# A four-layer sequence trunk: norm factors in PSUM and the state-space tables in wider products

## The chip, the cores and the metric

The kernel runs on one core of one Trainium2 chip. The metric is the device time of one execution in microseconds (us). Its engines each work through a queue of their own in order: TensorE (PE in the profile, PEld for its weight loads), VectorE (DVE), ScalarE (ACT), GpSimd (POOL) and SyncE (SP), which here issues the DMAs. All matmul products land in PSUM, eight banks of 2 KB per partition; everything else lies in SBUF.

## The reference

Four layers over a stream of 512 positions with 1024 channels, float32. Each layer has a token mixer (stick-breaking attention, a diagonal state-space layer, a convolution, attention again) and a SwiGLU channel mixer; each of these eight sub-layers stands between two RMS norms with scales and shifts computed from a conditioning vector.

```python
def rms_norm(x, g):
    y = xf * lax.rsqrt(jnp.mean(xf * xf, axis=-1, keepdims=True) + EPS)
    return y * g

for layer in range(DEPTH):
    sh_m, sc_m, g_m, sh_f, sc_f, g_f = split(mod_all[layer], 6)
    u = modulate(rms_norm(h, norm_g[layer, 0]), sh_m, sc_m)
    m = mixer(u)                       # attention, s5_layer or conformer_conv
    h = h + g_m * rms_norm(m, norm_g[layer, 1])
    u = modulate(rms_norm(h, norm_g[layer, 2]), sh_f, sc_f)
    f = (silu(u @ w_gate) * (u @ w_up)) @ w_down
    h = h + g_f * rms_norm(f, norm_g[layer, 3])

def s5_layer(u, ...):                  # 64 groups of 16 channels, 64 complex states each
    ar, ai = exp(lr*dt)*cos(li*dt), exp(lr*dt)*sin(li*dt)
    er, ei = ((a - 1) / lam)           # complex
    bb = e * b
    x[t] = a * x[t-1] + bb @ u[t]      # complex scan over the positions
    y = real(c @ x) + d_skip * u
    ...
```

## The kernel before, in words

**Layout.** The residual stream h lies in SBUF as eight chunks of 128 channels by 512 positions. A float32 product is made of three matmuls on a high and a low part of each operand (`mm3`, L219), both rounded for the fast format; the parts are made by ScalarE (a cast, L237) and by DVE or POOL (a subtraction, L238).

**Phases.** Each of the eight sub-layers is a phase: a first part (`first`), a body (`mid`), a last part (`last`), a norm of its input (`pre`) and of its output (`post`). `cross` (L296) leads from one phase to the next in two halves of 256 positions: while the norms of half A run, PE does the last blocks of half B; while the norms of half B run, it does the first blocks of the next phase on half A. The order of PE's matmuls there is written out by hand, and a norm says after how many microseconds of other PE work its own matmul stands (`yield wait`).

**Norms.** `add_square` (L433) squares a chunk on ScalarE and adds it to one of two sums, the even ones on DVE, the odd ones on POOL. `rstd` (L413) sums over partitions with a matmul of ones into a PSUM bank and makes the factor R in SBUF: a reciprocal root and a square on ScalarE, two instructions on DVE (L425, L427). `postnorm` (L470) scales each of eight chunks by R on DVE (L475) in place and adds it to h (L479), even chunks on DVE, odd ones on POOL. `pre_r` (L444) squares h again, and `prenorm` (L451) scales h by R into a scratch tile in SBUF (DVE, L462), from which ScalarE makes the high part (L463) and DVE the low part (L465) or, for odd chunks in a crossing, ScalarE and POOL (L467, L468).

**Tables.** The state-space layer works on four positions at a time with tables made of its parameters. They are made during the channel mixer of layer 0 (`ffn`, L482; its body is one dense run of 36 blocks of weights) and stored to DRAM. `s5_small` (L929) makes the 4096 values of a, e and of the rotations in a chain of small DVE instructions; `s5_tables(c)` (L1042) makes the tables of one of eight chunks: powers of a times B and C by repeated complex products on POOL (`cmul`, L1025; products L1035 to L1037 and L1039, sums L1038 and L1040), memsets and copies into block-diagonal tiles `bd` and `od` (ScalarE, L1072, L1073), eight transposes (L1077) and eight small matmuls (L1086) on PE, the rotation products on POOL, and seven stores on SyncE's queue (L1080, L1081, L1098, L1107).

**Order.** These tasks stand in a list (`todo`), together with 59 tasks of the conditioning (`mod_block`, L372: a 512 KB fetch and a DVE instruction L376), a table task at every fifth place (L1283); after each block of the body two tasks of the list are issued (`some`). But this is the program's order alone. The order in every engine's queue is set before the run by a planner with a model of durations (`TC`, L15), which takes at each step the instruction that is first in program order among those that it believes ready. At run time each engine follows that order, whatever comes late.

## Time and profile before

| | us |
|---|---|
| median of 3 runs | 2720.92 |
| lowest, highest | 2720.15, 2722.32 |
| the profiled execution | 2724.05 |
| its span, first to last instruction | 2722.3 |
| PE busy | 2480.0 |
| DVE, ACT, POOL busy | 1707.7, 1194.9, 798.1 |

The profiled execution is longer than its span by what lies around the first and last instruction. Busy time is an average over stages with different limits; the rows further down are taken from the stages that the change touches. "Idle before" is the time in which an engine stood still ahead of an instruction, with what released it. PEclk is the granted TensorE clock as a share of full speed.

### The profile page before, as it was taken

To read this page: it belongs to the slowest core of one execution; us is meant where nothing else is said; L and a number is where in the kernel's file an instruction comes from. 1 tells how busy PE (TensorE), PEld (TensorE's weight loads), DVE (VectorE), ACT (ScalarE), POOL (GpSimd) and SP (SyncE) were. 2 spreads that over 40 slices of the span, in tenths; PEclk is the share of its full clock that TensorE was granted. 3 is DMA by queue.
4 is the path that set the end of the run, shared out by engine and by line. 5 is a ranking of instruction groups with operands and counts; after the bars stand their busy time and mean duration, and the time that the engine had idled before them with its cause. 6 is when DMAs were issued, how large, how long until landed. Compare 5 with 4: busy or idle time off the path is not lost.

```text
span 2722.3 us, 35325 instructions
## 1 busy us (share of the span) xinstructions
PE 2480.0 (91%) x12903; PEld 2064.2 (76%) x12903; DVE 1707.7 (63%) x2693; ACT 1194.9 (44%) x2291; POOL 798.1 (29%) x1171
## 2 busy tenths in 40 slices
PE   7898999889866989999988879999998999899998
PEld 5676887666666888888876668888886777888887
DVE  8799767455469465555469986656364887632335
ACT  3577442433346454222356564222243776522222
POOL 4123314999825230000037752000021222300001
PEclk9999999998988999999989989999999999999999
DMA  7423226556636223755301211656221113122331
GB/s 257 149 92 107 76 89 215 174 195 208 233 115 187 69 86 113 235 184 193 127 30 39 70 63 47 224 200 233 96 91 62 40 43 103 42 93 93 93 100 56
DMA packets 115326, 335.09 MB, mean 123 GB/s; under 512 B 12112, under 2 KB 26960, under 8 KB 115152
## 3 DMA queue, kind: packets, MB, share of 16 engines
q1 hardware_dynamic: 115152, 332.84, 37.0%
q8 instruction: 101, 1.65, 0.2%
q14 instruction: 73, 0.60, 0.1%
HBM read 314.18 MB, written 18.61 MB: 122 GB/s over the span
## 4 chain that ended last, share of the span: by engine, by line
PE 61%; DVE 17%; POOL 11%; ACT 4%; issue 4%; DMA 2%; SPq 0%; DVEq 0%; POOLq 0%; ACTq 0%
PE mm L216 56%; PE aux L216 4%; DVE m L475 3%; DVE aux L812 2%; POOL x L1039 2%; POOL x L1037 2%; POOL x L1038 1%; POOL x L1040 1%; DVE raw L376 1%; DVE wlo L238 1%; POOL cm L1036 1%; DVE h L479 1%; POOL cm L1035 1%; PE aux L593 1%; DVE t L462 1%
## 5 line engine op out<-in xcount | busy, mean ns | idle before, releaser
L216 PE MATMUL mm<-u,whi 128*128 128x512 f32 (+1 forms) x3568 | 1078.7, 385 | 16.7 <-DVE cum L745 12.6
L216 PEld LDWEIGHTS mm<-u,whi 128*128 128x128 f32 x3568 | 659.6, 191 | 159.7 <-DVE cum L745 14.6
L237 ACT ACTIVATE whi<-raw 128x1024 fp32r<-128x1024 f32 (+3 forms) x392 | 344.3, 896 | 828.8 <-PE mm L216 519.0
L216 PE MATMUL mm<-u,wlo 128*128 128x512 f32 (+1 forms) x1784 | 687.3, 386 | 0.0
L238 DVE TENSOR_TENSOR wlo<-raw,whi 128x1024 fp32r<-128x1024 f32 (+2 forms) x302 | 357.8, 1187 | 394.8 <-ACT whi L237 391.6
L216 PE MATMUL mm<-hid,whi 128*128 128x512 f32 (+1 forms) x1832 | 506.3, 363 | 1.3 <-ACT whi L237 0.7
L216 PEld LDWEIGHTS mm<-u,wlo 128*128 128x128 f32 x1784 | 340.1, 191 | 70.0 <-issue 1.0
L216 PEld LDWEIGHTS mm<-hid,whi 128*128 128x128 f32 x1832 | 328.4, 191 | 60.2 <-issue 1.0
L216 PE MATMUL mm<-hid,wlo 128*128 128x512 f32 (+1 forms) x916 | 332.3, 364 | 1.8 <-DVE wlo L238 1.8
L441 POOL TENSOR_TENSOR accp<-accp,sq 128x256 f32<-128x256 f32 (+1 forms) x47 | 36.8, 784 | 817.8 <-ACT sq L440 817.5
L376 DVE SCALAR_TENSOR_TENSOR raw<-raw,cb 128x1024 f32<-128x1024 f32 x192 | 240.4, 1274 | 37.9 <-DMA raw<-in_w_modT_dram 36.8
L238 POOL TENSOR_TENSOR wlo<-raw,whi 128x512 fp32r<-128x512 f32 (+1 forms) x90 | 117.8, 1326 | 369.7 <-ACT whi L237 369.7
L495 DVE TENSOR_TENSOR g<-g,mm 128x512 f32<-128x512 f32 (+1 forms) x100 | 61.6, 622 | 253.8 <-PE mm L216 223.4
L216 PEld LDWEIGHTS mm<-hid,wlo 128*128 128x128 f32 x916 | 174.7, 191 | 29.9 <-DVE wlo L238 2.5
L216 PE MATMUL mm<-u,x 128*128 128x256 f32 (+1 forms) x832 | 130.0, 293 | 23.6 <-ACT u L463 8.8
L216 PE MATMUL mm<-hid,u 128*128 128x256 f32 x1104 | 143.3, 291 | 1.5 <-DVE m L757 1.5
L216 PEld LDWEIGHTS mm<-hid,u 128*128 128x128 f32 x1104 | 140.3, 199 | 2.6 <-DVE m L757 1.7
L216 PEld LDWEIGHTS mm<-u,x 128*128 128x128 f32 x832 | 113.9, 199 | 30.1 <-ACT u L463 10.7
L781 POOL TENSOR_TENSOR hid<-ident,hid 128x512 fp32r<-128x512 f32 (+1 forms) x17 | 18.5, 1108 | 315.1 <-ACT hid L237 311.6
L509 DVE TENSOR_TENSOR m<-mm,m 128x256 f32<-128x256 f32 (+1 forms) x92 | 47.7, 523 | 87.9 <-PE mm L216 87.9
L807 POOL TENSOR_TENSOR u<-u,t 128x512 f32<-128x512 f32 (+1 forms) x63 | 78.9, 1252 | 33.6 <-ACT t L806 30.6
L812 DVE SCALAR_TENSOR_TENSOR aux<-cum,vec,aux 128x512 f32<-128x512 f32 (+1 forms) x125 | 86.5, 708 | 2.5
(292 smaller groups left out, 3574.8 us busy)
## 6 DMA issues: line engine op xcount, KB each, us to landing
raw<-in_w_modT_dram SPq DMA_DIRECT2D x192, 512.0 KB, 4.4
raw<-in_ffn_w_gate_dram SPq DMA_DIRECT2D x88, 512.0 KB, 4.0
raw<-in_ffn_w_up_dram SPq DMA_DIRECT2D x88, 512.0 KB, 3.4
raw<-in_ffn_w_down_dram SPq DMA_DIRECT2D x64, 448.0 KB, 3.9
raw<-in_sb_w_qkv_dram SPq DMA_DIRECT2D x32, 512.0 KB, 3.4
raw<-in_ffn_w_down_dram SPq DMA_DIRECT2D x32, 512.0 KB, 4.6
raw<-in_cv_w_pw_dram SPq DMA_DIRECT2D x24, 512.0 KB, 3.3
s5tab<-x SPq DMA_DIRECT2D x40, 256.0 KB, 3.1
```

The source lines that it names most:

```text
L216: self.queue(self.nc.tensor.matmul(out, lhsT, rhs, **k))
L237: a = self.nc.scalar.activation(hi, src, AF.Copy)
L238: b = (self.nc.gpsimd if pool else self.nc.vector).tensor_tensor(lo, src, hi.bitcast(F32), ALU.subtract)
L376: self.after(nc.vector.scalar_tensor_tensor(raw, raw, 1.0, self.cb, ALU.mult, ALU.mult, accum_out=self.mod[l][:, e : e + 1]), self.mark)
L441: (nc.gpsimd if k % 2 and self.mark else nc.vector).tensor_tensor(acc, acc, sq, ALU.add)
L475: nc.vector.scalar_tensor_tensor(t, t, self.gpost[l][:, s, k : k + 1], R, ALU.mult, ALU.mult)
L495: self.mark = nc.vector.tensor_tensor(g, g, pu, ALU.mult)
L509: nc.vector.tensor_tensor(m[ob][:, sl], ps, m[ob][:, sl], ALU.add)
L807: nc.gpsimd.tensor_tensor(ap, ap, x, ALU.add)
L812: nc.vector.scalar_tensor_tensor(c, src(t), wd(k, t), c, ALU.mult, ALU.add)
L1037: TT(oim, are, bim, ALU.mult)
L1039: TT(ore, are, bre, ALU.mult)
```

## The change

It has three parts.

Norms: `rstd` leaves R in the PSUM bank of its sum and hands out the other half of that bank, into which `postnorm` puts the scaled chunk; all additions to h are DVE's. `prenorm` of a half takes a further PSUM bank (`room`) whose two halves hold the scaled chunks in turn; the second scratch of odd chunks stays in SBUF. `add_square` adds chunks 1 to 6 to one sum, on POOL, and leaves the square of chunk 7 by itself for the matmul of ones.

Tables: `s5_small` also makes four powers of a times e and of a; `s5_math` then makes each chunk's tables in two complex products of 256 elements and one of 512 in place of eight of 64 and four of 128. `bd`, `od` and `td` are cleared once and written again for each chunk; ScalarE sets the signs while it copies.

Order: the tables' work is split into `s5_math` (POOL), `s5_place` (ScalarE) and `s5_store` (PE, DVE, stores). The list has the math of chunk c+1 ahead of the placing of c, and the store of c after the math of c+2, just ahead of the placing of c+1. A table task stands at every third place instead of every fifth: 18 table tasks, 77 in all.

```diff
     def rstd(self, accs, n=S, wait=0, out=None):
+        nc = self.nc
+        bank = self.psum("aux")
+        ps = bank[:, :n]
...
         nc.vector.scalar_tensor_tensor(q, ps, EPS, q, ALU.add, ALU.mult)
-        out = r if out is None else out
+        out = ps if out is None else out
         self.step = square, nc.vector.scalar_tensor_tensor(out, q, -3.0, r, ALU.add, ALU.mult)
-        return out
+        return out, bank[:, n : 2 * n] if n < S else None
...
     def add_square(self, accs, src, k, sl=FULL):
-        acc = accs[k % 2][:, sl]
-        if k < 2:
-            return nc.scalar.activation(acc, src, AF.Square)
+        acc = accs[0][:, sl]
+        if k == 0 or k == KC - 1:
+            return nc.scalar.activation(accs[k > 0][:, sl], src, AF.Square)
         sq = self.scratch("sq", sl)
         square = nc.scalar.activation(sq, src, AF.Square)
-        (nc.gpsimd if k % 2 and self.mark else nc.vector).tensor_tensor(acc, acc, sq, ALU.add)
+        (nc.gpsimd if self.mark else nc.vector).tensor_tensor(acc, acc, sq, ALU.add)
         return square
...
     def prenorm(self, l, s, u, sl=FULL, before=None):
-        R = yield from self.pre_r(sl)
+        R, _ = yield from self.pre_r(sl)
+        n = sl.stop - sl.start
+        room = self.psum("aux") if n < S else None
         for k in range(KC):
...
-            t = self.scratch("t", sl)
+            t = self.scratch("t", sl) if room is None else room[:, k % 2 * n : (k % 2 + 1) * n]
             scale = nc.vector.scalar_tensor_tensor(t, self.h[:, k, sl], a, R, ALU.mult, ALU.mult)
             self.step = nc.scalar.activation(hi, t, AF.Identity, bias=b), scale
             if k % 2 == 0 or not self.crossing:
                 nc.vector.scalar_tensor_tensor(lo, t, b, hi.bitcast(F32), ALU.add, ALU.subtract)
             else:
-                nc.scalar.activation(t, t, AF.Identity, bias=b)
-                nc.gpsimd.tensor_tensor(lo, t, hi.bitcast(F32), ALU.subtract)
+                x = self.scratch("t", sl)
+                nc.scalar.activation(x, t, AF.Identity, bias=b)
+                nc.gpsimd.tensor_tensor(lo, x, hi.bitcast(F32), ALU.subtract)
...
     def postnorm(self, l, s, m, accs, sl=FULL, permuted=False):
-        R = yield from self.rstd([a[:, sl] for a in accs], sl.stop - sl.start, 1.6 if sl.start == 0 else 0.4)
+        R, t = yield from self.rstd([a[:, sl] for a in accs], sl.stop - sl.start, 1.6 if sl.start == 0 else 0.4)
         for k in range(KC):
-            t = m[k][:, sl]
-            nc.vector.scalar_tensor_tensor(t, t, self.gpost[l][:, s, k : k + 1], R, ALU.mult, ALU.mult)
+            nc.vector.scalar_tensor_tensor(t, m[k][:, sl], self.gpost[l][:, s, k : k + 1], R, ALU.mult, ALU.mult)
             h = self.h[:, k, sl]
             if permuted:
-                h, t = nat(h), perm(t)
-            (nc.gpsimd if k % 2 else nc.vector).tensor_tensor(h, h, t, ALU.add)
+                nc.vector.tensor_tensor(nat(h), nat(h), perm(t), ALU.add)
+            else:
+                nc.vector.tensor_tensor(h, h, t, ALU.add)
...
-            r = yield from self.rstd(sq, n, 5.0)
+            r, _ = yield from self.rstd(sq, n, 5.0)
...
-        nai = s("nai")
-        nc.vector.tensor_scalar(nai, ai, -1.0, None, ALU.mult)
-        self.s5p = dict(ar=ar, ai=ai, nai=nai, er=er, ei=ei, rho=rho, R0=R0, R1=R1)
+
+        pe, pa = ([t[:, i * P : (i + 1) * P].rearrange("p (j n) -> p j n", j=4) for i in range(2)]
+                  for t in (self.mx.tile([P, 2 * P], F32, tag="wt2", name=self.nm("pow"), bufs=2) for _ in range(2)))
+        for pw, at, step, ab in ((pe, 3, -1, (er, ei)), (pa, 0, 1, (ar, ai))):
+            for o, x in zip(pw, ab):
+                nc.gpsimd.tensor_scalar(o[:, at], x, 1.0, None, ALU.mult)
+            for j in range(3):
+                i, o = at + j * step, at + (j + 1) * step
+                self.cmul(pw[0][:, o], pw[1][:, o], pw[0][:, i], pw[1][:, i], ar, ai, [P, NPAIR])
+        x = lambda: self.chunk("x", F32)
+        bd, od, td = [x(), x()], [self.t512("cum", n=640), self.t512("cum", n=640)], x()
+        for t in (*bd, *od, td):
+            nc.gpsimd.memset(t, 0.0)
+        self.s5p = dict(rho=rho, R0=R0, R1=R1, pe=pe, pa=pa, bd=bd, od=od, td=td, made={})
...
     def cmul(self, ore, oim, are, aim, bre, bim, shape):
-        x = self.tmp.tile([P, 2, 256], F32, tag="u32", name=self.nm("cm"))
-        vw = [x[:, i, :n] for i in range(2)]
+        x = self.t512("u32")[:, :n]
...
+        if len(shape) == 4:
+            x = x.rearrange("p (a b c) -> p a b c", a=shape[1], b=shape[2])
+        TT(ore, are, bre, ALU.mult)
+        TT(x, aim, bim, ALU.mult)
+        TT(ore, ore, x, ALU.subtract)
         TT(oim, are, bim, ALU.mult)
-        TT(oim, oim, vw[1], ALU.add)
-        TT(ore, are, bre, ALU.mult)
-        TT(ore, ore, vw[0], ALU.subtract)
-
-    def s5_tables(self, c):
+        TT(x, aim, bre, ALU.mult)
+        TT(oim, oim, x, ALU.add)
+
+    def s5_math(self, c):
...
         tb = self.s5tab[c]
-        bcd = x()[:, :256]
+        bcd = self.mx.tile([P, 2 * P], F32, tag="w1", name=self.nm("bcd"))
         nc.sync.dma_start(bcd, ins["s5_bc"][c])
-        pw = x().rearrange("p (k j q c) -> p k j q c", k=2, j=4, q=4)
-        self.cmul(pw[:, 0, 3], pw[:, 1, 3], bv[:, 0], bv[:, 1], bc("er"), bc("ei"), SH)
-        for j in (2, 1, 0):
-            self.cmul(pw[:, 0, j], pw[:, 1, j], pw[:, 0, j + 1], pw[:, 1, j + 1], bc("ar"), bc("ai"), SH)
-        ow = [x()[:, :320].rearrange("p (l q c) -> p l q c", l=5, q=4) for _ in range(2)]
...
-        for l in range(1, 5):
-            self.cmul(ow[0][:, l], ow[1][:, l], ow[0][:, l - 1], ow[1][:, l - 1], bc("ar"), bc("nai"), SH)
+        if c % 2:
+            pw, ow = self.chunk("x", F32), self.chunk("x", F32)
...
+            pw, ow = (self.mx.tile([P, S], F32, tag=t, name=self.nm("pw")) for t in ("w3", "w02"))
+        SH = [P, 4, 4, 16]
+        for o, i, t in ((pw, 0, p["pe"]), (ow, 2, p["pa"])):
+            a = [bv[:, i + k].unsqueeze(1).to_broadcast(SH) for k in range(2)]
+            b = [t[k][:, :, 4 * c : 4 * c + 4].unsqueeze(3).to_broadcast(SH) for k in range(2)]
+            self.cmul(o[:, 0], o[:, 1], *a, *b, SH)
+        rt = [self.chunk("x", F32) for _ in range(2)]
+        rv = [t.rearrange("p (q a b) -> p q a b", q=4, a=8) for t in rt]
+        SH = [P, 4, 8, 16]
+        a = [p["R0"][k][:, 4 * c : 4 * c + 4, :].unsqueeze(2).to_broadcast(SH) for k in range(2)]
+        b = [p["R1"][k][:, 4 * c : 4 * c + 4, :].unsqueeze(3).to_broadcast(SH) for k in range(2)]
+        self.cmul(*rv, *a, *b, SH)
+        for k in range(2):
+            nc.sync.dma_start(tb[:, 5 + k, :], rt[k])
+        p["made"][c] = bv, pw, ow
+
+    def s5_place(self, c):
+
+        nc, p = self.nc, self.s5p
+        bv, pw, ow = p["made"].pop(c)
+        bd, od = p["bd"], p["od"]
...
         for k in range(2):
-            gp.memset(bd[k], 0.0)
-            gp.memset(od[k], 0.0)
             for g in range(2):
                 rows = slice(g * 64, g * 64 + 64)
+                sign = -1.0 if k else 1.0
                 nc.scalar.activation(bdv[k][rows, :, :, g, :], pw[rows, k].rearrange("p j q c -> p q j c"), AF.Copy)
-                nc.scalar.activation(odv[k][rows, :, :, g, :], ow[k][rows].rearrange("p l q c -> p q l c"), AF.Copy)
+                nc.scalar.activation(odv[k][rows, :, 0, g, :], bv[rows, 2 + k], AF.Copy, scale=sign)
+                nc.scalar.activation(odv[k][rows, :, 1:5, g, :], ow[rows, k].rearrange("p l q c -> p q l c"), AF.Copy,
+                                     scale=sign)
+
+    def s5_store(self, c):
+
+        nc, p = self.nc, self.s5p
+        tb = self.s5tab[c]
+        bd, od, td = p["bd"], p["od"], p["td"]
...
         for k in range(2):
             pt = self.psum("aux")
             for q in range(4):
                 nc.tensor.transpose(pt[:, q * P : (q + 1) * P], bd[k][:, q * P : (q + 1) * P], self.ident)
-            ti = x()
+            ti = self.chunk("x", F32)
             nc.scalar.activation(ti, pt, AF.Copy)
             nc.sync.dma_start(tb[:, k, :], ti)
             nc.sync.dma_start(tb[:, 2 + k, :].rearrange("p (q m) -> p q m", q=4),
...
-        td = x()
-        gp.memset(td, 0.0)
...
         nc.sync.dma_start(tb[:, 4, :], td)
-        rt = [x(), x()]
-        rv = [t.rearrange("p (q a b) -> p q a b", q=4, a=8) for t in rt]
-        for q in range(4):
-            self.cmul(rv[0][:, q], rv[1][:, q], b0(0), b0(1), b1(0), b1(1), [P, 8, 16])
-        for k in range(2):
-            nc.sync.dma_start(tb[:, 5 + k, :], rt[k])
...
-        return [self.s5_small] + [lambda c=c: self.s5_tables(c) for c in range(KC)]
+        def layout(c):
+            if c:
+                self.s5_store(c - 1)
+            if c < KC:
+                self.s5_place(c)
+
+        math = [lambda c=c: self.s5_math(c) for c in range(KC)]
+        lay = [lambda c=c: layout(c) for c in range(KC + 1)]
+        return [self.s5_small, math[0]] + [f for x in zip(math[1:], lay) for f in x] + lay[-2:]
...
                 for t in own + self.mod_tasks(l + 1, 0) + self.mod_tasks(l + 1, 1):
-                    if tabs and len(self.todo) % 5 == 0:
+                    if tabs and len(self.todo) % 3 == 0:
                         self.later(tabs.pop(0))
                     self.later(t)
             p.mid()
```

## Rows read from the trace of the kernel before

**Rows 1.** The profile page, part 1: busy us, share of the span, instructions.

```profile
PE 2480.0 (91%) x12903; PEld 2064.2 (76%) x12903; DVE 1707.7 (63%) x2693; ACT 1194.9 (44%) x2291; POOL 798.1 (29%) x1171
```

**Rows 2.** Windows: stretch, us, busy us (instructions) per engine, PEclk, DMA; last two L1077, L1086.

```profile
346.80:774.95 428.15, 389.56 (x1840) 315.01 (x1840) 244.95 (x460) 154.36 (x263) 300.10 (x679) 0.96 0.56 187
1023.79:1369.61 345.82, 345.41 (x1649) 286.20 (x1648) 178.53 (x264) 107.78 (x154) 6.83 (x8) 1.00 0.51 169
...
346.80:774.95 428.15, 12.91 (x64) 8.49 (x64) 0.96 0.56 187
...
346.80:774.95 428.15, 18.66 (x128) 13.54 (x128) 0.96 0.56 187
```

**Rows 3.** Windows, same columns: the table stretch, and ten us inside it.

```profile
470.00:730.00 260.00, 224.12 (x976) 173.66 (x975) 134.85 (x178) 97.11 (x169) 259.92 (x610) 0.94 0.57 188
605.00:615.00 10.00, 2.69 (x11) 2.17 (x11) 5.82 (x9) 3.76 (x7) 10.00 (x25) 0.73 0.98 342
```

**Rows 4.** Waits, 470 to 730 us: total us, times, longest; last SyncE's, 346 to 830.

```profile
ACT x L1072 <- POOL x L1040: 61.3, 8, 10.5
ACT cum L1073 <- POOL x L1040: 29.8, 8, 7.7
PE aux L1077 <- ACT x L1072: 27.3, 8, 7.2
...
SPq L1107 <- POOL x L1040: 55.5, 8, 11.0
```

**Rows 5.** Timeline, SyncE and ScalarE: start us, us, instruction, [idle before <- releaser].

```profile
603.88 0.33 SPq L1107 DMA_DIRECT2D s5tab<-x  x1
605.27 0.38 SPq L178 DMA_DIRECT2D raw<-in_ffn_w_down_dram  x1
...
610.20 0.95 ACT L237 ACTIVATE whi<-raw 128x896 fp32r<-128x896 f32 x1 [15.85 <-DMA raw<-in_ffn_w_down_dram]
```

**Rows 6.** Windows: sum and mean over the eight crossings between sub-layers.

```profile
sum 401.30, PE 278.93 PEld 260.68 DVE 318.63 ACT 215.60 POOL 184.96; mean PE 34.87 PEld 32.59 DVE 39.83 ACT 26.95 POOL 23.12
```

**Rows 7.** Timeline of POOL: products (L1039, L1035), sums (L1040), 256 and 64 wide.

```profile
439.83 0.63 POOL L1039 TENSOR_TENSOR x<-x,x 128x256 f32<-128x256 f32 x1
443.57 0.73 POOL L1040 TENSOR_TENSOR x<-x,cm 128x256 f32<-128x256 f32 x1
...
476.30 0.29 POOL L1035 TENSOR_TENSOR cm<-x,s5nai 128x64 f32<-128x64 f32 x1
476.80 0.32 POOL L1040 TENSOR_TENSOR x<-x,cm 128x64 f32<-128x64 f32 x1
```

**Rows 8.** Chain of waits, pieces in order of time: start us, us, what.

```profile
800.70 0.73 POOL accp L441
...
804.60 4.66 DVE m L475 x8
...
812.99 0.97 DVE acch L441
...
814.01 2.09 PE aux L216 x4
...
1416.00 1.67 DVE t L462 x4
```

**Rows 9.** DVE's groups by form in 2310 to 2354 us: xcount | busy us, mean ns.

```profile
L475 DVE SCALAR_TENSOR_TENSOR m<-m,gpost,u 128x256 f32<-128x256 f32 x16 | 12.0, 814 | 0.0
...
L479 DVE TENSOR_TENSOR h<-h,m 128x256 f32<-128x256 f32 x8 | 4.8, 644 | 0.0
...
L425 DVE SCALAR_TENSOR_TENSOR u<-aux,u 128x256 f32<-128x256 f32 x3 | 1.2, 417 | 1.8 <-ACT u L424 1.8
```

**Rows 10.** ScalarE's groups by form in the same stretch.

```profile
L463 ACT ACTIVATE u<-t,mod 128x256 fp32r<-128x256 f32 x12 | 5.6, 499 | 2.4 <-DVE t L462 2.2
...
L467 ACT ACTIVATE t<-t,mod 128x256 f32<-128x256 f32 x6 | 3.0, 504 | 0.2
```

**Rows 11.** Timeline of PE: 84 matmuls of 256 columns in a run.

```profile
1357.57 10.24 PE L216 MATMUL mm<-hid,u 128*128 128x256 f32 x84
```

More of the change, by code (lines that the diff above doesn't have):

```diff
@@ L416, in rstd @@
         nc = self.nc
-        ps = self.psum("aux")[:, :n]
+        bank = self.psum("aux")
+        ps = bank[:, :n]
         yield wait
@@ L931, in s5_small @@
         tiles = {}
-        KEEP = ("ar", "ai", "nai", "eer", "eei", "rho")
+        KEEP = ("rho",)
         room = [self.chunk("x", F32) for _ in range(2)]
@@ L1030, in cmul @@
             n *= d
-        x = self.tmp.tile([P, 2, 256], F32, tag="u32", name=self.nm("cm"))
-        vw = [x[:, i, :n] for i in range(2)]
+        x = self.t512("u32")[:, :n]
         if len(shape) == 3:
-            vw = [y.rearrange("p (a b) -> p a b", a=shape[1]) for y in vw]
-        TT(vw[0], aim, bim, ALU.mult)
-        TT(vw[1], aim, bre, ALU.mult)
+            x = x.rearrange("p (a b) -> p a b", a=shape[1])
+        if len(shape) == 4:
+            x = x.rearrange("p (a b c) -> p a b c", a=shape[1], b=shape[2])
@@ L1037, in cmul @@
+        TT(ore, are, bre, ALU.mult)
+        TT(x, aim, bim, ALU.mult)
+        TT(ore, ore, x, ALU.subtract)
         TT(oim, are, bim, ALU.mult)
-        TT(oim, oim, vw[1], ALU.add)
-        TT(ore, are, bre, ALU.mult)
-        TT(ore, ore, vw[0], ALU.subtract)
-    def s5_tables(self, c):
+        TT(x, aim, bre, ALU.mult)
+        TT(oim, oim, x, ALU.add)
+    def s5_math(self, c):
         nc, ins, p = self.nc, self.ins, self.s5p
-        gp = nc.gpsimd
-        pr = slice(4 * c, 4 * c + 4)
-        SH = [P, 4, 16]
-        bc = lambda name: p[name][:, pr].unsqueeze(2).to_broadcast(SH)
-        x = lambda: self.chunk("x", F32)
@@ L1058, in s5_tables @@
[L1058 to L1064 removed]
+        if c % 2:
+            pw, ow = self.chunk("x", F32), self.chunk("x", F32)
+        else:
+            pw, ow = (self.mx.tile([P, S], F32, tag=t, name=self.nm("pw")) for t in ("w3", "w02"))
@@ new lines, in s5_math @@
+        pw, ow = (t.rearrange("p (k j q c) -> p k j q c", k=2, j=4, q=4) for t in (pw, ow))
+        SH = [P, 4, 4, 16]
[5 more added lines that the diff above has]
+        rv = [t.rearrange("p (q a b) -> p q a b", q=4, a=8) for t in rt]
@@ L1067, in s5_tables @@
         for k in range(2):
-            gp.memset(bd[k], 0.0)
-            gp.memset(od[k], 0.0)
             for g in range(2):
                 rows = slice(g * 64, g * 64 + 64)
+                sign = -1.0 if k else 1.0
                 nc.scalar.activation(bdv[k][rows, :, :, g, :], pw[rows, k].rearrange("p j q c -> p q j c"), AF.Copy)
-                nc.scalar.activation(odv[k][rows, :, :, g, :], ow[k][rows].rearrange("p l q c -> p q l c"), AF.Copy)
+                nc.scalar.activation(odv[k][rows, :, 0, g, :], bv[rows, 2 + k], AF.Copy, scale=sign)
[5 more added lines that the diff above has]
+        bd, od, td = p["bd"], p["od"], p["td"]
+        bdv = [t.rearrange("p (q j g c) -> p q j g c", q=4, j=4, g=2) for t in bd]
+        odv = [o.rearrange("p (q l g c) -> p q l g c", q=4, l=5, g=2) for o in od]
         for k in range(2):
```

7 lines of the change are left out of this document (removed).

## The prediction

> **What bounds the kernel now.** I read the page first: TensorE (PE) is busy for 2480.0 of 2722.3 us [rows 1], so at most some 240 us of waiting and what a lowered clock costs are to be had. The change touches two places where PE waits; I priced each from its own stretch.
>
> The first is the channel mixer of layer 0. The windows table sets it beside the same stretch of layer 1, which does the same matmuls without tables: 428.15 us against 345.82, so building the tables costs 82.3 us. Of this 12.91 + 18.66 = 31.6 us are the tables' own matmuls; PE's idle time is 38.6 against 0.4 us, so 38.2 us are waiting; the remaining 12.6 us are a lower granted clock, 0.96 against 1.00 [rows 2]. The clock falls where PE has just stood still: 0.73 of full speed, a mix of its two levels, in 605 to 615 us, with PE busy for 2.69 us of ten [rows 3]. Loss to be won: 50.8 us. What PE waits for, the waits view tells: GpSimd (POOL) is busy without a pause from 470 to 730 us [rows 3], ScalarE's copies L1072 and L1073 wait for it 61.3 and 29.8 us, and PE's transposes wait for those copies, eight times, up to 7.2 us [rows 4]. SyncE's queue passes the delay on: at 603.88 us it issues a store of the rotation tables (these stores wait for POOL 55.5 us in all, eight times [rows 4]), the weight fetch stands behind that store, and ScalarE's cast of that weight at 610.20 us has waited 15.85 us for the DMA; the table copies are queued behind the cast [rows 5].
>
> The second place is the norms at the eight crossings. Together these stretches are 401.3 us with PE busy for 278.9 [rows 6]; 122 us idle, though the convolution's own norm and the state-space turn account for part. Within one half-norm of them nothing but VectorE (DVE) and POOL works: scaling starts at 804.60 us, and PE's sum of squares follows at 814.01 [rows 8].
>
> **Tables: POOL's work.** Before, one chunk of tables is 48 products and sums of 64 elements, 24 of 128, two copies and five memsets; after, 12 of 256 and 6 of 512, and no memset. The number of elements is the same, so what goes is the fixed part of each instruction. Clean rows: 0.29 and 0.32 us at 64 (product, sum), 0.63 and 0.73 us at 256 [rows 7]; their slope gives 1.08 and 1.28 us at 512, an estimate. One chunk: 8 x 0.63 + 4 x 0.73 + 4 x 1.08 + 2 x 1.28 = 14.8 us clean. Now it is 259.9 / 8 = 32.5 us [rows 3], of which by the same prices (64 wide 48 x 0.3 = 14.4; 128 wide, interpolated, 24 x 0.43 = 10.3; the rest 3.4; less 0.04 us of overlap each) about 25 us are clean, and 7.5 us, 23%, are waits for DVE. With the same share: 14.8 / 0.77 = 19.2 us a chunk, 154 us in place of 260. POOL then ends near 470 + 154 = 624 us rather than near 728; the powers (six products of 32 elements, 36 instructions of some 0.25 us, 9 us) lie in its idle time before 470.
>
> **Tables: what PE still waits.** The queues' order is fixed before the run; PE waits by as much as POOL comes later than planned. Now that is 38.2 / 8 = 4.8 us a chunk, 15% of POOL's chunk time. If the same 15% of 19.2 us stays, 2.9 x 8 = 23 us stay; if the extra chunk between math and PE's part covers it, nothing. This extra chunk is only worth its name where POOL is ahead of the program; while POOL is the last (it starts late, behind the serial chain of `s5_small`), the planner can place PE's part as soon as its inputs are due. I take the middle, 11 us, and a quarter of the clock's 12.6, 3 us: 50.8 - 14 = **37 us won**, bounds 0 to 51. The moved part also brings its DMAs: the stores of `od` stand in SyncE's queue one chunk later, and ScalarE's `s5_place` now overwrites `od` and `bd` in place, so it waits for these stores and for PE's reads; queued behind it are ScalarE's casts of weights, and PE waits for these. Before, the memsets on POOL took that wait. `bcd` has one buffer now, so a chunk's fetch waits for the placing before it; POOL's rotation product (about 9 us) covers that placing (twelve copies) and fetch. I cost both at nothing; without this cover some 5 us a chunk come back.
>
> **Norms.** R, the scaled product and the prenorm's product go to PSUM; all additions to h go to DVE; all additions of squares but the last go to POOL, and the last square needs none. DVE: 16 instructions of 256 elements a half instead of 12. Alone such an instruction takes 0.42 us, whether it reads two SBUF operands (1.67 us for four) [rows 8] or PSUM (417 ns) [rows 9]. Beside POOL it takes 814 ns when it scales and 644 ns when it adds [rows 9]: in these rows the two engines alternate wherever both DVE operands lie in SBUF. After, each has one SBUF operand; I take 0.42 to 0.45 us, 6.7 to 7.2 us for 16, then one square (0.42 us) and its hand-over: 7.4 us at the middle in place of 9.4. The last addition on POOL before each sum, 0.73 us [rows 8], goes where PE waits for it. Together 2.5 us a half, about 14 halves with PE waiting (the first half of the last crossing is covered and the last half ends in the output's DMAs): 35 us. POOL's chain of six additions at 0.73 us keeps up with h, which comes every 0.84 us; what it gains in additions it loses in h's. Bounds 0 to 45; I take 34.
>
> Against this stands the prenorm's `room`: two halves of one bank, which DVE writes and ScalarE reads. No row of before shows two engines at different columns of one bank at one time, so the cost is bounded. Lower end nothing. Upper end: strict turns. A pair of chunks then takes DVE 3 x 0.45, ScalarE 3 x 0.50 [rows 10] and six hand-overs of 0.04: 3.1 us, where ScalarE alone needs 1.5 and PE consumes a pair in 24 x 0.122 = 2.9 us [rows 11] (18 matmuls, 2.2 us, into attention). In the first halves PE has the old blocks to do meanwhile. In the six second ones the excess over PE's own pace shows, 0.2 x 4 x 5 + 0.9 x 4 = 8 us, or at most all of it, 6 x 4 x 1.6 = 38. I take 12 us off, near the lower sum: **22 us won**.
>
> [...]
>
> **Sum.** Profiled execution 2724.05 us - 37 - 22 = 2665; it stood 3.1 us over the median of 2720.92, so in medians 2662. I say **2662 us**. Five `mod_block` tasks now come after the last block of the first mixer (77 tasks, 72 slots): under 3 us, in the range.
>
> **Rivals.** (a) Both gains whole: PE's part always finds its inputs, turns don't show. 2720.9 - 51 - 34 = 2636. For it: POOL's load falls by 40%; against: 470 us stays its start. 15%. (b) The waits move: POOL starves on `bcd`, or SyncE's order holds the weights up as now; tables give 8, norms 22: 2691. For it: the 15.85 us wait [rows 5]. 13%. (c) The turns in `room` show in full, 38 us against 34 won; tables 30: 2695. For it: ScalarE's three instructions of 0.50 us a pair [rows 10] cannot overlap DVE's then. 7%; together with (b), tables 8: 2717, 5%. [...] 4%. [...] (e) Slower: `s5_place` at ScalarE's head waits for `od`'s store, with the weight casts behind it. It decides from 50.8 / 8 + 22 / 8 = 9 us of PE waiting a chunk; at 11 us a chunk, tables cost 88 - 51 = 37 more and norms return 22: 2736. For it: queue waits of 15.85 us exist. Against: the store's inputs are complete a chunk earlier. 6%.
>
> **How the numbers follow.** Forecast 50%, spread 2640 to 2682. (a) reaches down to 2625, (b), (c) and (d) up to 2705. The range 2628 to 2705 leaves out (e), (b) with (c), and the edge of (a). About 0.2% (5.4 us) is what a measurement of this kernel can tell from no change. Faster by more 89%, within 5% ((b) with (c)), slower 6% ((e)).
>
> **What would show it.** The mixer of layer 0 near 390 us instead of 428; POOL's cmul lines at 256 and 512 wide, some 19 us a chunk, ended by 640 us; L1077's successors waiting under 2 us each; the scalings of the postnorm at 0.42 to 0.48 us instead of 0.81; no POOL wait ahead of a norm's sum. Wrong, if scalings stay above 0.6 us, if ScalarE's waits for DVE inside the prenorm grow past 2 us a pair on the chain, or if PE's waits in 470 to 640 us still sum to 30 us.

## The result and the profile after

The changed kernel takes **2692.61 us** (median of 4 runs, 2691.46 to 2693.86) beside 2721.62 us (2720.15 to 2724.05) for the kernel before on the same chip: 29.0 us less, ratio 0.989 [0.9878, 0.9902]. The forecast was 2662 us, 59 us less, with a range of 2628 to 2705. The sign and the range held; half of the forecast gain did not come.

The two profiled executions differ by 2722.3 - 2689.7 = 32.6 us of span. PE's busy time hardly moves, DVE's and POOL's fall (part 1 of the page of after, to be read beside [rows 1]):

```profile
PE 2475.5 (92%) x12903; PEld 2064.0 (77%) x12903; DVE 1649.7 (61%) x2662; ACT 1199.7 (45%) x2323; POOL 682.5 (25%) x757
```

To see where the time went, cut both spans at the same events: the matmul of ones that sums the squares of half A of an output, and the one that sums those of half B of the next input. Between these two lies most of a crossing. For the seven crossings that lead from one sub-layer to the next that gives, in the windows of the kernel before (stretch, length, busy us of each engine, PEclk, DMA share, GB/s; the first crossing and the sum of the seven):

```profile
306.40:345.67 39.27, 31.76 (x237) 30.37 (x235) 34.36 (x65) 20.53 (x48) 20.63 (x23) 0.96 0.08 28
...
sum 288.79, PE 216.84 PEld 205.93 DVE 242.86 ACT 151.78 POOL 144.31; mean PE 30.98 PEld 29.42 DVE 34.69 ACT 21.68 POOL 20.62
```

and in those of the kernel after:

```profile
312.80:347.95 35.15, 31.14 (x237) 29.20 (x235) 26.51 (x64) 21.09 (x52) 19.26 (x24) 1.00 0.10 31
...
sum 266.11, PE 217.32 PEld 205.41 DVE 192.53 ACT 155.64 POOL 129.75; mean PE 31.05 PEld 29.34 DVE 27.50 ACT 22.23 POOL 18.54
```

The first crossing starts at 312.80 us instead of 306.40: 6.4 us are lost before any norm of a crossing has run. The windows of after for the two mixers that [rows 2] show:

```profile
349.10:761.40 412.30, 379.27 (x1840) 309.32 (x1840) 251.57 (x456) 157.10 (x289) 187.04 (x239) 0.96 0.59 194
...
1004.90:1350.70 345.80, 345.11 (x1645) 285.90 (x1644) 177.90 (x257) 106.00 (x152) 8.91 (x11) 1.00 0.51 169
```

| stretch | after less before, us | forecast |
|---|---|---|
| start to the first crossing's sum | +6.4 | 0 |
| seven crossings, sum to sum | -22.7 | -22 |
| mixer of layer 0, with the edges to these sums | -15.7 | -37 |
| everything else | -0.6 | 0 |
| span | -32.6 | -59 |

So the norms' sum came out as forecast, the tables gave less than half, and one loss was not in the sum at all. What PE still waits for in the mixer of layer 0, by the waits view of after, 349 to 761 us (engine, operation, what it waited for: us in total, times, longest):

```profile
PE aux L1112 <- ACT x L1097: 11.4, 8, 3.5
PE mm L216 <- ACT hid L237: 9.4, 1, 9.4
PE mm L216 <- ACT whi L237: 7.8, 1, 7.8
PE aux L1121 <- ACT cum L1099: 1.9, 4, 0.8
PE mm L216 <- DVE hid L238: 1.6, 1, 1.6
```

With two smaller lines these make the 33.0 us by which the stretch is longer than PE is busy. 13.3 us of them (L1112 and L1121) are the tables' matmuls waiting for ScalarE's placing, and behind it POOL: the wait that the forecast spoke of, at 11 us. The two large single waits, 9.4 us at 583 us and 7.8 + 1.6 us at 729 to 739 us, are others.

**The wait at 583 us** is a chain through two queues (timeline of after, SyncE and ScalarE: start, us, instruction, [idle before <- releaser]):

```profile
578.40 0.33 SPq L375 DMA_DIRECT2D raw<-in_w_modT_dram  x1
589.58 2.80 SPq L1083 DMA_DIRECT2D s5tab<-x  x2
592.94 0.40 SPq L178 DMA_DIRECT2D raw<-in_ffn_w_down_dram  x1
...
591.69 0.60 ACT L1114 ACTIVATE x<-aux 128x512 f32<-128x512 f32 x1 [8.50 <-DMA s5tab<-x]
592.19 0.62 ACT L237 ACTIVATE hid<-g 128x512 fp32r<-128x512 f32 x1
```

SyncE stands still from 578.7 to 589.6 us, since the store of the rotation tables (L1083) waits for POOL's product. At ScalarE's head the copy of a transposed table (L1114) wants a buffer that such a store has to free first; behind it in the queue stands the cast of `hid` for which PE waits, from 583.50 to 592.86 us. L1114 waits for such stores five times in this stretch, 26.3 us in all; PE's wait follows from this one. POOL, for its part, is idle for 12.14 us behind PE's wait, not ahead of it: the single buffer `bcd` of its next chunk can be fetched only when the placing, delayed by the same copy, has read it (timeline of after, POOL):

```profile
604.16 0.62 POOL L1052 TENSOR_TENSOR pw<-bcd,pow 128x256 f32<-128x256 f32 x1 [12.14 <-DMA bcd<-in_s_bc_dram]
...
617.23 1.10 POOL L1053 TENSOR_TENSOR u<-x,x 128x512 f32<-128x512 f32 x1
618.41 1.28 POOL L1054 TENSOR_TENSOR x<-x,u 128x512 f32<-128x512 f32 x1
```

**The wait at 731 us** is one for weights that stand behind eight fetches of the conditioning (timeline of after, SyncE, ScalarE, PE):

```profile
714.96 16.79 SPq L375 DMA_DIRECT2D raw<-in_w_modT_dram  x8
732.95 10.47 SPq L178 DMA_DIRECT2D raw<-in_ffn_w_down_dram  x7
...
737.76 0.95 ACT L237 ACTIVATE whi<-raw 128x896 fp32r<-128x896 f32 x1 [3.50 <-DMA raw<-in_ffn_w_down_dram]
...
738.76 0.79 PE L216 MATMUL mm<-hid,whi 128*128 128x256 f32 x2 [7.80 <-ACT whi L237]
```

**The loss at the start** sits in one gap (timeline of after, PE, then DVE):

```profile
60.69 0.80 PE L216 MATMUL aux<-whi,u 128*128 128x512 f32 x1 [8.24 <-DVE t L466]
...
59.88 0.75 DVE L466 SCALAR_TENSOR_TENSOR t<-h,apre,aux 128x512 f32<-128x512 f32 x1
```

The very first norm runs over all 512 positions and now leaves R in a bank of the `aux` group. The first projection keeps eight accumulators, all eight banks of the program's two groups. The last of them cannot begin until the scaling of the last chunk (59.88 to 60.63 us) has read R, and all its matmuls come at the end.

**One half-norm** answers to [rows 8] (timeline of after, DVE, POOL, ScalarE, PE):

```profile
789.88 0.49 DVE L479 SCALAR_TENSOR_TENSOR aux<-m,gpost,aux 128x256 f32<-128x256 f32 x1
790.41 0.42 DVE L484 TENSOR_TENSOR h<-h,aux 128x256 f32<-128x256 f32 x1
790.86 0.49 DVE L479 SCALAR_TENSOR_TENSOR aux<-m,gpost,aux 128x256 f32<-128x256 f32 x1
...
797.29 0.72 POOL L443 TENSOR_TENSOR acch<-acch,sq 128x256 f32<-128x256 f32 x1 [0.19 <-ACT sq L442]
...
797.72 0.42 ACT L440 ACTIVATE accph<-h 128x256 f32<-128x256 f32 x1 [0.56 <-DVE h L484]
...
798.07 1.22 PE L216 MATMUL aux<-acch,ones_d 128*128 128x256 f32 x2 [10.11 <-POOL acch L443]
```

A chunk takes DVE 0.98 us, eight take 7.8 us, and from the first scaling to the sum it is 798.07 - 789.88 = 8.19 us instead of 9.41. POOL's last addition ends at 798.01 and the last square at 798.14 us: they come together, POOL does keep up.

### The profile page after: what moved, and what is told of

Its sections match the earlier page's. It is cut to its first block, busy times and chain, and to the rows that moved or that the text cites. A ratio compares the mean times of both kernels' runs of the same rounds, so it can differ in the third digit from the quotient of the medians.

```text
span 2689.7 us, 34961 instructions
## 1 busy us (share of the span) xinstructions
PE 2475.5 (92%) x12903; PEld 2064.0 (77%) x12903; DVE 1649.7 (61%) x2662; ACT 1199.7 (45%) x2323; POOL 682.5 (25%) x757
## 5 line engine op out<-in xcount | busy, mean ns | idle before, releaser
L443 POOL TENSOR_TENSOR acc<-acc,sq 128x256 f32<-128x256 f32 (+1 forms) x92 | 72.1, 783 | 871.9 <-ACT sq L442 870.4
L443 POOL TENSOR_TENSOR acch<-acch,sq 128x256 f32<-128x256 f32 x96 | 75.4, 785 | 58.2 <-ACT sq L442 56.7
L817 DVE SCALAR_TENSOR_TENSOR aux<-cum,vec,aux 128x512 f32<-128x512 f32 (+1 forms) x125 | 86.6, 709 | 2.6
```

What stands on the lines that cost most here:

```text
L443: (nc.gpsimd if self.mark else nc.vector).tensor_tensor(acc, acc, sq, ALU.add)
L817: nc.vector.scalar_tensor_tensor(c, src(t), wd(k, t), c, ALU.mult, ALU.add)
```

## The experiments

Each run was made beside the kernel before on the same chip; times are medians, and differences are taken from 2692.6 us unless another kernel is named. The runs stem from several chips, on which the kernel before took 2719.9 to 2722.6 us, and the interval of each ratio reaches some 4 us to either side; so a difference of 5 us or less is uncertain in size. Where it matters, the gain over the change is also given as the difference of the two distances from the kernel before.

**The two parts alone.** First the changed kernel with `rstd`, `add_square`, `prenorm` and `postnorm` of before:

```diff
-        out = ps if out is None else out
+        out = r if out is None else out
...
-            t = self.scratch("t", sl) if room is None else room[:, k % 2 * n : (k % 2 + 1) * n]
+            t = self.scratch("t", sl)
```

> The tables' part of the change with the norms of before. Theory (stages of the two traces: the mixer of layer 0 is 15.7 us shorter after): 2722 - 16 = 2706 us, the mixer of layer 0 near 412 us, crossings and start as before. Rival, my forecast's term (37 us, with norms that disturb the mixer's order and eat the difference): 2685 us, the mixer near 391 us. Rival, the gain in the mixer needs the norms' change: 2715 or more.

Measured 2711.38 us, ratio 0.9958 [0.9942, 0.9975]: 10.6 us less than the 2722.0 us of before beside it. Then the kernel before with the new norms:

> The norms' part of the change with the tables of before. Theory: the crossings give 20 us, the start loses 6 us (a PSUM bank held by R keeps one of the eight accumulators of the first projection waiting): 2722 - 14 = 2708 us, the mixer of layer 0 as before at 428 us. Rival, the crossings' gain comes partly from the tables being out of the way (only the first crossings could tell): less than 10 us won, 2712 or more. Rival, my forecast's term with no loss at the start: 2700 us.

Measured 2707.53 us, 0.9945 [0.993, 0.996]: 14.4 us less. The parts add up to 25 of 29 us; the 4 us between them lie within the intervals, so neither help nor hindrance is shown. In the traces the mixer of layer 0 goes from 428.15 to 414.15 us with the tables alone and stays at 428.70 us with the norms alone; the seven crossings sum to 287.13 us with the tables alone and 267.76 us with the norms alone. The forecast's 37 us for the tables is out by itself, not through the norms.

**R of the first norm back in SBUF.**

```diff
-        out = ps if out is None else out
+        out = (ps if n < S else r) if out is None else out
```

> The changed kernel, but the norm over all 512 positions at the start leaves R in SBUF, as before the change. Theory (R's bank is the eighth that the first projection's accumulators need): the wait of 8.24 us at 52 us goes, 2692.6 - 6.5 = 2686 us. Rival, the start is late for another reason (all squares on one engine's chain, another order of the first fetches): 2692 us, the wait stays.

Measured 2686.55 us, 0.9869 [0.9855, 0.9884], 6.1 us less; no wait above 1.5 us is left between 50 and 62 us. By the distances from the kernel before it is 6.4 us (35.4 against 29.0). The profiled execution is the longest of the four (2691.4 us): its first crossing starts at 307.65 instead of 312.80 us, but later stretches take the 5.2 us back, 3.0 of them in the state-space layer; the others took 2684.7 to 2686.9 us. So the bank was the cause of the wait, and the norms' part without it is 14.4 + 6.1 = 20.5 us, beside 22 forecast.

**R of the halves back in SBUF**, the product still in PSUM.

```diff
-        out = ps if out is None else out
+        out = (r if n < S else ps) if out is None else out
```

> The changed kernel, but the norms of halves leave R in SBUF; the scaled products stay in PSUM. Theory (VectorE and GpSimd alternate where both VectorE operands lie in SBUF): the postnorm's scalings go from 0.49 us back to 0.65 us or more beside GpSimd's additions, 8 x 0.2 = 1.6 us a half or more, most of the crossings' gain is lost: 2705 us or more. Rival, the gain came from GpSimd having less to do (no additions to h), not from where R lies: scalings at 0.42 to 0.50 us and 2685 to 2693 us.

Measured 2722.69 us, 1.0011 [1.0001, 1.002]: 30 us more. DVE's groups by form in one crossing of after (2279 to 2316 us) and of this kernel (2306 to 2350 us), to be read beside [rows 9] (xcount | busy us, mean ns | idle before):

```profile
L479 DVE SCALAR_TENSOR_TENSOR aux<-m,gpost,aux 128x256 f32<-128x256 f32 x16 | 7.8, 486 | 0.3
L484 DVE TENSOR_TENSOR h<-h,aux 128x256 f32<-128x256 f32 x16 | 6.7, 418 | 0.4
```

```profile
L479 DVE SCALAR_TENSOR_TENSOR aux<-m,gpost,u 128x256 f32<-128x256 f32 x16 | 10.6, 661 | 0.3
L466 DVE SCALAR_TENSOR_TENSOR aux<-h,apre,u 128x256 f32<-128x256 f32 x9 | 6.7, 746 | 1.1 <-ACT t L472 0.9
L484 DVE TENSOR_TENSOR h<-h,aux 128x256 f32<-128x256 f32 x16 | 6.7, 417 | 0.4
```

The same instruction with the same output takes 661 ns where `m` and R both lie in SBUF and 486 ns where R lies in PSUM, and the additions, which read one SBUF operand in both kernels, stay at 417 and 418 ns. The sum of the seven crossings goes back up:

```profile
sum 287.29, PE 220.73 PEld 205.79 DVE 220.34 ACT 156.53 POOL 132.56; mean PE 31.53 PEld 29.40 DVE 31.48 ACT 22.36 POOL 18.94
```

21.2 of the 22.7 us are gone. So the norms' gain is the place of R, not the smaller load on POOL. Sorted by what POOL does meanwhile, the same trace also names the partner: the 46 scalings of the postnorms beside which POOL stands still take 491 ns, the 82 others 694 ns in the mean and up to 1614 ns. With R in PSUM, in after, the two groups take 487 and 486 ns. Of the other 9 us of the 30, 4.9 lie in the mixer of layer 0 (418.3 against 413.4 us from sum to sum); their cause was not looked for.

**The turns in `room`.**

```diff
-        room = self.psum("aux") if n < S else None
+        room = [self.psum("aux") for _ in range(2)] if n < S else None
...
-            t = self.scratch("t", sl) if room is None else room[:, k % 2 * n : (k % 2 + 1) * n]
+            t = self.scratch("t", sl) if room is None else room[k % 2][:, :n]
```

> The changed kernel, but the prenorm of a half puts its scaled chunks into two PSUM banks in turn instead of two halves of one. Theory (VectorE and ScalarE take turns in the one bank, a pair of chunks lasts 2.95 us, but TensorE has other blocks meanwhile; it waits less behind the second halves' sums than before the change): the pairs get shorter, to 2.4 us or less, and the time stays at 2692 us, within 3. Rival, my forecast's term (the turns cost 12 us): 2681 us.

Measured 2698.1 us, 0.9906 [0.9892, 0.9919]: 5.5 us more (4.5 by the distances from the kernel before), not less. DVE's scalings of a prenorm in after, then here (timeline):

```profile
1009.83 0.49 DVE L466 SCALAR_TENSOR_TENSOR aux<-h,apre,aux 128x256 f32<-128x256 f32 x1 [0.91 <-ACT t L472]
...
1014.28 0.49 DVE L466 SCALAR_TENSOR_TENSOR aux<-h,apre,aux 128x256 f32<-128x256 f32 x1 [0.91 <-ACT t L472]
...
1017.23 0.49 DVE L466 SCALAR_TENSOR_TENSOR aux<-h,apre,aux 128x256 f32<-128x256 f32 x1 [0.91 <-ACT t L472]
```

```profile
1009.55 0.88 DVE L466 SCALAR_TENSOR_TENSOR aux<-h,apre,aux 128x256 f32<-128x256 f32 x2
...
1011.10 0.88 DVE L466 SCALAR_TENSOR_TENSOR aux<-h,apre,aux 128x256 f32<-128x256 f32 x2
```

In one bank DVE waits for ScalarE's read of the other half; a pair lasts 1017.23 - 1014.28 = 2.95 us. In two banks it lasts 1.55 us. The turns are real, but taking them away brings nothing: TensorE has other blocks to do meanwhile. In the 15 us that begin 0.8 us behind the input's sum of half B, PE is busy for 86.8 of 105 us over the seven crossings of after, for 86.6 in the kernel before, which has no such turns, and for 88.8 here. The releaser in the rows is a semaphore, so here the program itself keeps the turns; one bank without them was not tried. Why two banks are slower is not settled; the seven crossings sum to 268.61 us here, 2.5 us more than in after, and in the one that enters layer 3 the output's sum of half B comes 8.5 us behind the input's sum of half A instead of 7.1. That prenorm A, no longer held up, goes ahead of half B's work on DVE is argued from the timeline, not shown.

**The queue in the tables.** First the copy of the transposed table gets a tile of its own:

```diff
-            ti = self.chunk("x", F32)
+            ti = self.t512("t")
             nc.scalar.activation(ti, pt, AF.Copy)
```

> The changed kernel, but the transposed table is copied to a scratch tile of its own instead of one of the rotating tiles that also hold the rotation products. Theory (the copy at ScalarE's head waits for the store of a rotation product, that store waits for GpSimd, and a cast that TensorE needs stands behind the copy): the wait of 9.36 us at 583 us goes, 2692.6 - 9 = 2683 us. Rival, the same store stands ahead of the weight fetches in SyncE's queue, so TensorE waits there instead: 2691 us or more, a wait of 6 us or more between 580 and 605 us with a weight's cast behind it.

Measured 2692.69 us, 0.9891 [0.9876, 0.9905]: nothing won, as the rival said. The wait moved one queue on (timeline of this kernel, ScalarE, then SyncE):

```profile
576.54 0.58 ACT L1114 ACTIVATE t<-aux 128x512 f32<-128x512 f32 x1
577.02 0.62 ACT L237 ACTIVATE hid<-g 128x512 fp32r<-128x512 f32 x1
...
596.48 0.95 ACT L237 ACTIVATE whi<-raw 128x896 fp32r<-128x896 f32 x1 [8.75 <-DMA raw<-in_ffn_w_down_dram]
...
588.86 2.84 SPq L1083 DMA_DIRECT2D s5tab<-x  x2
592.27 0.41 SPq L178 DMA_DIRECT2D raw<-in_ffn_w_down_dram  x1
```

`hid` is cast at once, but the weight fetch stands behind the rotation stores as before. Next these stores were issued a list entry later, with the placing:

```diff
-        for k in range(2):
-            nc.sync.dma_start(tb[:, 5 + k, :], rt[k])
-        p["made"][c] = bv, pw, ow
+        p["made"][c] = bv, pw, ow, rt
...
+        bv, pw, ow, rt = p["made"].pop(c)
+        for k in range(2):
+            nc.sync.dma_start(self.s5tab[c][:, 5 + k, :], rt[k])
```

> The changed kernel with the transposed table copied to a scratch tile of its own, and in addition the two stores of a chunk's rotation products issued with the placing of that chunk, one list entry later, instead of right behind the product. Theory (in the run with the scratch tile alone TensorE's wait only moved from ScalarE's copy to the weight fetch that stands behind these stores in SyncE's queue): now neither stands behind the product, the waits of 7.7 us between 595 and 605 us go, 2692.6 - 8 = 2684 us. Rival, TensorE waits for GpSimd's tables by another way (the transposes, four copies later): 2691 us or more, transposes waiting 8 us or more in all around 600 us.

Measured 2692.99 us, 0.99 [0.9885, 0.9915]: nothing again, PE's waits for weights in the stretch are 9.5 us for `whi` and 7.0 us for `wlo`. My theory fell, and its rival named the time but not the place: the stores stand at the same place in SyncE's queue (two of them at 591.14 us, the weight fetch at 594.55 us). The list's order did not move them; that the planner places them by its belief about POOL is argued, not shown.

**Two buffers for the fetched factors.**

```diff
-        bcd = self.mx.tile([P, 2 * P], F32, tag="w1", name=self.nm("bcd"))
+        bcd = self.t512(("acch", "accph")[c % 2], n=2 * P, bufs=1)
```

> The changed kernel with two buffers in place of one for the fetched factors of a chunk. Theory (GpSimd's 12.1 us of idle time at 592 us comes from this buffer, but TensorE's largest wait comes from SyncE's queue): GpSimd ends near 630 us instead of 642, TensorE's waits of 3.5 and 1.5 us behind it at 631 to 638 us shrink, 2689 us. Rival, my prediction's case of the waits that move (the one buffer is what holds the tables back): 2675 us or less. Rival, GpSimd's idle time costs nothing: 2692 us.

Measured 2685.67 us, 0.9874 [0.986, 0.9889]: 6.9 us less (5.2 by the distances from the kernel before), between theory and rival, nearer to the theory. The mixer's window and its waits on PE:

```profile
351.70:755.00 403.30, 375.73 (x1840) 306.86 (x1839) 251.64 (x456) 155.86 (x293) 187.87 (x239) 0.98 0.59 198
```

```profile
PE aux L1112 <- ACT x L1097: 11.3, 7, 3.5
PE mm L216 <- ACT whi L237: 7.8, 1, 7.8
PE aux L1121 <- ACT cum L1099: 3.2, 2, 2.3
```

9.0 us shorter than in after: 5.5 us less waiting (27.6 against 33.0) and 3.5 us less PE busy with the same matmuls (granted clock 0.98 against 0.96). The wait of 9.4 us for `hid` is gone, but not because the queues wait less for POOL there (timeline of this kernel, SyncE and ScalarE):

```profile
595.24 0.33 SPq L1083 DMA_DIRECT2D s5tab<-x  x1
...
585.05 0.61 ACT L237 ACTIVATE hid<-g 128x512 fp32r<-128x512 f32 x1
...
597.54 0.60 ACT L1114 ACTIVATE x<-aux 128x512 f32<-128x512 f32 x1 [11.56 <-POOL u L1056]
```

The store of the rotation product is issued later than in after (595.24 against 589.58 us), and the copy L1114 waits longer (11.56 against 8.50 us). But the cast of `hid` now stands ahead of that copy in ScalarE's queue, and the weight casts do too. POOL, without its idle time on `bcd`, ends at 631 instead of 641 us. How much of the gain is the buffer and how much the other order that came with it stays open.

**The extra chunk taken back.**

```diff
         def layout(c):
-            if c:
-                self.s5_store(c - 1)
             if c < KC:
                 self.s5_place(c)
+                self.s5_store(c)
```

> The changed kernel, but TensorE's part of a chunk's tables stands right behind its placing in the list, not behind the next chunk's products. Theory (GpSimd is the last in the whole stretch, and the planner puts TensorE's part where it believes the inputs ready, whatever the list's distance): within 4 us of 2692 us. Rival, my forecast's step (the extra chunk covers about half of the 23 us that TensorE would wait): 2701 us or more, transposes waiting 20 us or more in all.

Measured 2691.84 us, 0.9882 [0.9868, 0.9895]: no difference. The tables' matmuls wait 12.3 + 4.3 us instead of 11.4 + 1.9. The third part of the change, TensorE's share one more chunk later, brings nothing that can be measured.

**The left-over tasks.**

```diff
-            self.some(rate)
+            self.some(rate + (i >= more))
...
-            self.dense(todo, rate)
+            self.dense(todo, rate, more=30 if l == 0 else 99)
```

> The changed kernel with three tasks instead of two behind each of the last six blocks of the first mixer, so that no task is left over at its end. Theory (five left-over fetches of 512 KB stand ahead of the next weights, which TensorE awaits 7.8 us at 731 us): that wait goes, and the clock that falls behind it: 2692.6 - 8.5 = 2684 us. Rival, the transfers themselves are at their limit there, in whatever order: the wait moves to an earlier block, 2690 us or more.

Measured 2687.62 us, 0.988 [0.9866, 0.9895]: 5.0 us less (3.2 by the distances from the kernel before). PE's wait for `whi` shrinks from 7.8 to 3.5 us; the rest stays, with six fetches of the conditioning still in a row ahead of the weights. Both theory and rival hold in part.

**The three mends together**, then with the rotation stores issued by POOL itself (`nc.gpsimd.dma_start` in place of `nc.sync.dma_start` at L1083).

> The changed kernel with three mends together: R of the norm at the start in SBUF (won 6.1 us alone), two buffers for the fetched factors (6.9 us), three tasks behind each of the last six blocks of the first mixer (5.0 us). Theory (three separate waits of TensorE): the gains add up, 2692.6 - 18 = 2675 us. Rival, the second and the third overlap (a shorter mixer only shifts its load onto its end): 2680 us or more.

Measured **2674.49 us** (5 runs), ratio to before 0.9815 [0.9802, 0.9829]: 18.1 us less than the change as made, where the three alone give 6.1 + 6.9 + 5.0 = 18.0. By the distances from the kernel before it is 19.1 against 14.8, so that they add up is shown within some 4 us. This kernel beats both.

> The kernel with the three mends, and the stores of the rotation products issued by GpSimd itself, on a queue of its own, behind its products. Theory (what is left is SyncE's queue, in which these stores hold weight fetches until GpSimd arrives, while the list's order does not matter): the weight casts' waits for DMA in the mixer shrink, 2675 - 5 = 2670 us. Rival, with two buffers for the factors the weights are no longer late, and GpSimd pays for issuing 16 stores: 2675 us or more.

Measured 2679.01 us, 0.9841 [0.9824, 0.9858]: not faster; 4.5 us slower by the medians, with intervals that just meet. SyncE no longer waits for these stores (31.2 us in all with the three mends, 0 now), but PE's waits in the mixer are 27.7 us against 23.7, and DVE is busy 271.18 us there against 249.18. The two profiled executions are about equally long (2677.09 and 2678.32 us), so the traces don't show where the 4.5 us go. My theory fell: with the buffers doubled, these stores no longer hold what PE needs.

## Why the prediction was right where it was, and wrong where it was

**Norms, 22 us: right in sum, wrong in both terms.** The mechanism, DVE and POOL alternating where both operands of DVE lie in SBUF, is shown by moving R alone (661 against 486 ns a scaling) and by sorting the scalings (694 ns beside POOL against 491 without it). In the trace of before the delay goes both ways: a scaling beside one of POOL's subtractions of 512 elements takes 1.51 us (2310.38 us) instead of 0.48, and a POOL product of 64 elements beside one of DVE's of 1024 takes 1.36 us (480.22 us) instead of 0.29. But the forecast's 34 us rested on 0.42 to 0.45 us an instruction. The 0.42 us of a scaling was the length of a run of four, 1.67 us [rows 8], divided by four, but these overlap; each takes 0.48 us, with both operands in SBUF and POOL idle (lines view of before, 1415.9 to 1417.7 us):

```profile
L462 DVE SCALAR_TENSOR_TENSOR t<-h,apre,u 128x256 f32<-128x256 f32 x4 | 1.7, 480 | 0.1
```

After the change a scaling takes 0.49 us and a pair with its dependent addition 0.98 us, so that the path from scaling to sum saves 1.22 us a half where 2.0 of the 2.5 us were to come from. Over 14 halves the crossings gained 22.7 / 14 = 1.6 us each. The 12 us taken off for the turns were not spent: the turns come in full (2.95 us a pair; the upper bound said 3.1), and PE's busy time behind the second halves' sums does not show them. Two errors of about 12 us cancelled: that 22 us came out is luck.

**A term that was missing.** R of the first norm holds a bank that eight accumulators need: 6.1 us. The prediction looked for the cost of PSUM in the `room` of the halves and never counted banks in the one norm that runs over all positions.

**Tables, 37 us: the mis-sized step.** POOL's part was right: 157.1 us from 470 us on, 19.6 us a chunk (forecast 19.2), prices of 0.62, 1.10 and 1.28 us as estimated. Some 9 us of it are the powers, which the forecast had put ahead of 470 us. It ends at 641 us instead of 624, mostly for the 12.1 us on `bcd`. The waits of the tables' own matmuls came out near the forecast, 13.3 us (forecast 11), in part by luck: the extra chunk was to halve them and took 3.3 us off (16.6 without it). What failed are the two items costed at next to nothing. "I cost both at nothing" was said of ScalarE's and SyncE's queues and of the single buffer; the queues returned 9.4 us in one place, where the copy L1114, waiting for a store that waits for POOL, stood ahead of a cast that PE needs. A second buffer removed that wait, but by another order of ScalarE's queue; that the single buffer caused it is not shown. "Under 3 us" was said of the five left-over tasks; the waits there are 7.8 + 1.6 us, and spreading the tasks gave 5.0. The clock (0.96 against 1.00 in layer 1) kept 7.4 us, forecast 3: the mixer is 412.3 - 345.8 = 66.5 us longer than that of layer 1, less 32.3 us of idle time (33.0 against 0.7) and 26.8 us of the tables' own matmuls (lines view of after, 349 to 761 us):

```profile
L1121 PE MATMUL aux<-cum,x 128*32 128x128 f32 x128 | 16.8, 283 | 1.9 <-ACT cum L1099 1.9
L1112 PE MATMUL aux<-ident,x 128*128 128x128 f32 x64 | 10.0, 288 | 11.4 <-ACT x L1097 11.4
```

Together 32.3 + 7.4 = 39.7 us of loss remain where 14 were forecast. That 15.8 us were won and not 50.8 - 39.7 = 11.1 comes from the tables' own matmuls, which the forecast left at 31.6 us: they take 26.8.

**The rivals.** Rival (b), "the waits move", with its 13%, named both places (POOL starving on `bcd`, SyncE's order holding the weights) and gave 8 us for the tables and 2691 us; the tables alone gave 10.6 us. It deserved more than the forecast: [rows 5] showed the same chain at work before, and the change left all its links in place, the store behind POOL's product, the weight behind the store. (c) fell: the turns do not show. (d), whose 4% stands in the forecast's range, put an extra price on PSUM for DVE that no run shows: while POOL stands still, a scaling takes 478 ns in SBUF alone (before) and 487 ns with two operands in PSUM (after), 0.01 us more, and an addition that reads PSUM takes 416 ns (after) where one from SBUF takes 424 (before). (e) did not occur at `s5_place`, but its kind, a copy at ScalarE's head waiting for a store, did at L1114.

**The signs.** Mixer near 390 us: 412. POOL's chunks near 19 us: yes. The successors of L1077 waiting under 2 us each: 1.4 us in the mean, but up to 3.5. ScalarE's waits for DVE in the prenorm below 2 us a pair: 10.3 us for the eight pairs in 975 to 1025 us, 1.3 us a pair. Scalings at 0.42 to 0.48 us: 0.49. No POOL wait ahead of a norm's sum: POOL's chain is named there, but ends with the last square. PE's waits in 470 to 640 us still summing to 30: 22.7 us in 470 to 645 us (175.00 less 152.32 busy), the rest at the mixer's end.

## What to carry to other kernels

When an engine is made faster, follow each queue that passed its delay on, and ask which link of that chain the change really removes; an item costed at nothing needs its own cover named by a row. Count buffers and banks where a value changes its place: one bank at the start cost 6.1 us, and a second 1 KB buffer, with the other order that it brought, was worth 6.9, beside the 29 that were won. Read a duration from one row and not from a run of overlapping ones divided by their number. Before adding distance to a program's list, look whether the list or the planner sets the queue's order; here the distance did nothing, twice.

## What the runs showed of the hardware

While POOL stood still, the time of a DVE instruction of 256 elements went by its kind, and hardly by PSUM (means of all such rows of a trace). A scaling, which also reads one value per channel, takes 478 ns from SBUF into SBUF (before, L462 and L475) and 487 ns with R and the product in PSUM (after, L466 and L479). An addition takes 424 ns from SBUF (before, L479) and 416 ns with one operand in PSUM (after, L484). The last instruction of R, which has no such value, takes 424 ns into SBUF (before, L427) and 432 ns into PSUM (after, L429). That the value per channel makes the difference, 54 to 71 ns, is read from these rows; no edit tested it.

While POOL worked, a postnorm's scaling with both operands in SBUF took 798 ns in the mean (before, 109 of 128), with one in PSUM 486 ns (after, 82 of 128).

Two independent scalings followed each other at 0.39 us (0.88 us for two, each of 0.49; the run with two banks, 1009.55 us); a dependent addition started 0.53 us after its scaling (after, 789.88 and 790.41 us).

Issuing 16 stores from POOL cost POOL 9.5 us (0.59 us each), and DVE was busy 22 us longer in the mixer of layer 0 (271.18 against 249.18 us): its splits of weights, all operands in SBUF, went from 1330 to 1476 ns, while its products that read PSUM stayed at 639 ns. Whether the issuing or a changed overlap with POOL's products does that stays open.

Where PE had stood still, the clock fell: 0.57 of full speed in 730 to 740 us (after), with PE busy for 1.63 us of ten. It is a mix of the two levels that the traces of before and after show, 1.00 and 0.50; in 732 to 744 us the granted clock was 0.50, in 745 to 760 us 1.00 again:

```profile
730.00:740.00 10.00, 1.63 (x5) 0.91 (x5) 8.38 (x18) 1.62 (x3) 0.00 (x0) 0.57 0.91 316
```
